# RMSNorm on one core: loads and stores in fewer, larger transfers, three of them split into 27 and 5 rows, with the direction changes tied to landings

## The chip, the cores and the metric

The kernel runs on one core of a Trainium2 chip. The metric is device time in microseconds (us); lower is better. All transfers go over one hardware queue that SyncE (SP in the profile) feeds and that 16 DMA engines serve. The compute is split over ScalarE (ACT), VectorE (DVE) and GpSimd (POOL); TensorE (PE) only spreads gamma over the partitions once.

## What is computed

```python
def setup_inputs():
    batch, seq, dim = 16, 1024, 512
    return {"x": np.random.randn(batch, seq, dim).astype(np.float32),
            "gamma": np.ones(dim, dtype=np.float32)}

def reference(x, gamma):
    eps = 1e-5
    rms = np.sqrt(np.mean(x ** 2, axis=-1, keepdims=True) + eps)
    return (x / rms * gamma).astype(np.float32)
```

There are 16384 rows of 512 floats, 33.55 MB in and 33.55 MB out. Every row is divided by its own root mean square and multiplied by gamma.

## The kernel before

The 16384 rows are four tiles of 128 partitions x 32 rows x 512 floats. A "row" below is one row on every partition: 128 x 2 KB = 256 KB. Partition p of a tile holds 32 consecutive rows of x, so a transfer of n rows moves n x 2 KB of contiguous memory for each partition. There are three SBUF slots (64 KB a partition each); tiles 0, 1, 2 and 3 use slots 0, 1, 2 and 0 (`slot_of`). The results overwrite x in its slot, so tile 3 can only be loaded when tile 0 has been stored.

The work goes in groups of rows, written as `(tile, first row, rows, pieces, POOL's share)`. For each group:

- `square_sums` (L89 to L99): for each piece, ACT squares the rows into a scratch (L96) and DVE sums over the 512 columns (L97). A piece of 9 rows uses rows 23 to 31 of slot 2 as its scratch, as long as tile 2 is not there. Other pieces alternate between a PSUM scratch of 7 rows and an SBUF scratch of 5.
- `inverse_rms` (L101 to L104): ACT takes the root of sum/512 + eps (L102), DVE the reciprocal (L103).
- `scale_by_pool` (L106 to L113): POOL does the last `share` rows of the group by itself, first times the reciprocal (L109), then times gamma (L110).
- `scale` (L115 to L118): ACT multiplies the other rows by their reciprocals, one instruction a row.
- `times_gamma` (L120 to L127): DVE multiplies the same rows by gamma, in one instruction (L122).

The schedule is written by hand: each engine runs its instructions in the order of the program. The main loop (L166 to L182) goes one group ahead: while group k is scaled, group k + 1 is squared and summed; the reciprocals of group k + 1 follow the gamma product of group k on DVE.

All DMAs are issued by SP in the order of the program: `load` (L45), `store` (L49) and gamma's pieces (L58). The loads of tile 0 and half of tile 1 come first, then each group's `transfers` (L129 to L149). SP waits at each for what it needs: a load into a slot for the last readers of those rows, a store for DVE's and POOL's results. While SP waits, every later transfer waits with it, but the DMA engines go on with what is already queued.

Of the kernel before, what the change touches and what calls it, by code (L numbers as in the profile page):

```python
# [9 lines left out]
def kernel(  # L10
# [14 lines left out]
    of = out.flatten_outer_dims()  # L25
    N, D = xf.shape
# [17 lines left out]
    def load(t, slot, r0, r1):  # L44
        dma = nc.sync.dma_start(out=slots[slot][:, r0:r1], in_=xv[t][:, r0:r1])  # L45
        before_scale.append((slot, r0, r1, dma))

    def store(t, slot, r0, r1):
        dma = nc.sync.dma_start(out=ov[t][:, r0:r1], in_=slots[slot][:, r0:r1])  # L49
        before_scale.append((slot, r0, r1, dma))  # L50

    gamma_row = const.tile([1, D], fp32)
    pieces = (0, 128, 224, 320, 416, D)

    load(0, 0, 0, 1)
    load(0, 0, 1, 8)
    for c0, c1 in zip(pieces, pieces[1:]):
        nc.sync.dma_start(out=gamma_row[:, c0:c1], in_=gamma.unsqueeze(0)[:, c0:c1])  # L58
    load(0, 0, 8, 16)
    load(0, 0, 16, 32)  # L60
    load(1, 1, 0, 16)

    ones_col = const.tile([1, P], fp32)
    nc.gpsimd.memset(ones_col, 1.0)  # L64
# [9 lines left out]


    groups = [
        (0, 0, 7, (7,), 3),
        (0, 7, 9, (9,), 5),
        (0, 16, 16, (7, 9), 7),
        (1, 0, 16, (7, 9), 7),  # L80
        (1, 16, 16, (7, 5, 4), 7),
        (2, 0, 16, (7, 5, 4), 7),
        (2, 16, 16, (7, 5, 4), 7),
# [36 lines left out]
    def times_gamma(t, g, r0, r1):  # L120
# [4 lines left out]
        for slot, b0, b1, earlier in before_scale:  # L125
            if slot == slot_of[t] and b0 < g + r1 and g + r0 < b1:
                tc.declare_no_dep(scaled.ins, earlier.ins, reason="ScalarE waited for it before it scaled these rows")  # L127

    def transfers(t, g):  # L129
        if (t, g) == (0, 0):  # L130
            store(0, 0, 0, 1)
            load(1, 1, 16, 32)
            store(0, 0, 1, 2)
            load(2, 2, 0, 23)
        elif (t, g) == (0, 16):
            store(0, 0, 2, 3)
            load(2, 2, 23, 32)
            store(0, 0, 3, 16)
            store(0, 0, 16, 32)
            load(3, 0, 0, 16)  # L140
            load(3, 0, 16, 32)
        elif (t, g) == (1, 16):
            store(1, 1, 0, 32)
        elif (t, g) == (2, 16):
            store(2, 2, 0, 32)
        elif (t, g) == (3, 0):
            store(3, 0, 0, 16)
        elif (t, g) == (3, 16):
            store(3, 0, 16, 32)  # L149
# [16 lines left out]
    for k, group in enumerate(groups):  # L166
        t, g, n, pieces, share = group
        mine = n - share
        half = (mine + 1) // 2
        ahead = groups[k + 1 :][:1]  # L170
        ss, todo = pieces_of(ahead[0]) if ahead else (None, [])
        scale_by_pool(rstd, t, g, n, share)
        for piece in todo[:2]:
            square_sums(*piece)
        scale(rstd, t, g, 0, half)
        for piece in todo[2:]:
            square_sums(*piece)
        scale(rstd, t, g, half, mine)
        times_gamma(t, g, 0, mine)
        transfers(t, g)  # L180
        for nxt in ahead:
            rstd = inverse_rms(ss, nxt[2])  # L182
# [30 lines left out]
```

## Time and profile before

| | |
|---|---|
| time, median of 3 runs | 161.68 us (161.65 to 161.87) |
| span of the profiled execution, first to last instruction | 160.2 us (160.165) |
| bytes moved | 67.12 MB, a mean of 419 GB/s over the span |
| busy share | DVE 70%, ACT 67%, POOL 66%, PE 1% |
| busy share of the 16 DMA engines | 98.1% |
| DMA packets | 2747 |

The profiled execution's own time is not given apart from its span; the median of the runs is 1.5 us above the span, which is what lies before the first and after the last instruction. In the profile, "idle before, releaser" says how long an engine stood still before an instruction and what ended it. In the windows the columns are the window and its length, then busy time and number of instructions of PE, PEld (weight load), DVE, ACT and POOL, the clock granted to TensorE, the busy share of the DMA engines and the GB/s that they moved. In the timeline the columns are start, duration, engine, line, operation, and output from input; SPq are the DMA issues of SP.

### The profile page before, as it was taken

Reading aid. Unit: us, or ns where it says so; the run is one execution under the profiler, and the core shown is the slowest. Engines: PE = TensorE matmul, PEld = TensorE weight load, DVE = VectorE, ACT = ScalarE, POOL = GpSimd, SP = SyncE. Lnnn points to the kernel's source line nnn. Section 1 sums busy time; section 2 is a strip of 40 time slices with the busy share of each in tenths; the row PEclk is TensorE's granted clock in tenths of the full one; section 3 lists DMA queues with packets and bytes.
Section 4 is the critical chain, followed back from the end, with each engine's and each line's share of the span. In section 5 each row is a group of like instructions: output and inputs, shape, how many; then the busy total and the mean of one; then the engine's idle time right before and its main releaser. Section 6 shows DMA issues by size and latency. Waiting matters only on the chain.

```text
span 160.2 us, 276 instructions
## 1 busy us (share of the span) xinstructions
PE 2.0 (1%) x2; PEld 0.5 (0%) x2; DVE 112.0 (70%) x39; ACT 107.8 (67%) x108; POOL 106.4 (66%) x24
## 2 busy tenths in 40 slices
PE   0050000000000000000000000000000000000000
PEld 0010000000000000000000000000000000000000
DVE  0018098899798999999999999999999009700000
ACT  3071967976999998999899899989960990000000
POOL 1000951994999599999999999999999980000000
DMA  5999999899999899999999999996996996999994
GB/s 189 431 421 475 442 401 458 340 446 491 417 435 494 388 379 383 426 450 475 434 401 426 483 401 393 524 491 295 524 491 295 524 491 295 401 491 417 401 450 196
DMA packets 2747, 67.12 MB, mean 419 GB/s; under 512 B 313, under 2 KB 314, under 8 KB 826
## 3 DMA queue, kind: packets, MB, share of 16 engines
q1 hardware_dynamic: 2746, 67.11, 98.1%
q14 instruction: 1, 0.01, 0.0%
HBM read 33.56 MB, written 33.55 MB: 419 GB/s over the span
## 4 chain that ended last, share of the span: by engine, by line
DVE 59%; ACT 22%; DMA 4%; ACTq 0%; issue 0%; SPq 0%
DVE ss L97 36%; DVE slot L122 23%; ACT slot L118 8%; ACT slot L96 7%; ACT sq_psum L96 6%; DMA slot<-in_x_dram 4%; DVE ss L103 1%; ACT ss L102 1%; ACTq L208 0%; ACT gamma_b L165 0%; SPq L45 0%; ACTq L96 0%
## 5 line engine op out<-in xcount | busy, mean ns | idle before, releaser
L109 POOL TENSOR_TENSOR slot<-slot,ss 128x3584 f32<-128x3584 f32 (+2 forms) x9 | 47.0, 5218 | 24.1 <-DVE ss L103 24.1
L110 POOL TENSOR_TENSOR slot<-slot,gamma_b 128x3584 f32<-128x3584 f32 (+2 forms) x9 | 59.3, 6587 | 0.7
L97 DVE TENSOR_REDUCE ss<-sq_psum 128x7 f32<-128x3584 f32 (+1 forms) x13 | 42.2, 3247 | 13.7 <-ACT sq_psum L96 13.7
L118 ACT ACTIVATE slot<-slot,ss 128x512 f32<-128x512 f32 x75 | 47.3, 706 | 4.7 <-DVE ss L103 4.7
L122 DVE TENSOR_TENSOR slot<-slot,gamma_psum 128x4608 f32<-128x4608 f32 (+2 forms) x9 | 41.3, 4590 | 8.7 <-ACT slot L118 8.7
L96 ACT ACTIVATE sq_psum<-slot 128x3584 f32<-128x3584 f32 (+1 forms) x13 | 34.6, 2658 | 6.4 <-DMA slot<-in_x_dram 5.7
L97 DVE TENSOR_REDUCE ss<-slot 128x9 f32<-128x4608 f32 x3 | 14.9, 4954 | 4.4 <-ACT slot L96 4.2
L97 DVE TENSOR_REDUCE ss<-sq_sbuf 128x5 f32<-128x2560 f32 x5 | 14.0, 2803 | 0.0
L96 ACT ACTIVATE slot<-slot 128x4608 f32<-128x4608 f32 x3 | 12.1, 4033 | 0.0
L96 ACT ACTIVATE sq_sbuf<-slot 128x2560 f32<-128x2560 f32 x5 | 11.6, 2321 | 0.0
L102 ACT ACTIVATE ss<-ss,eps_t 128x16 f32<-128x16 f32 (+2 forms) x9 | 2.7, 305 | 11.9 <-DVE ss L97 11.9
L103 DVE RECIPROCAL ss<-ss 128x16 f32<-128x16 f32 (+2 forms) x9 | 2.1, 236 | 0.4 <-ACT ss L102 0.4
L66 PE MATMUL gamma_psum<-gamma_row,ones_col 1*128 1x512 f32 x2 | 2.0, 1122 | 8.6 <-DMA gamma_row<-in_gamma_dram 8.6
L72 ACT ACT_TABLE_LOAD x1 | 1.3, 1283 | 1.2 <-PEq L197 1.2
L165 ACT COPY gamma_b<-gamma_psum 128x512 f32<-128x512 f32 x1 | 0.6, 567 | 0.0
L66 PEld LDWEIGHTS gamma_psum<-gamma_row,ones_col 1*128 1x128 f32 x2 | 0.5, 308 | 8.6 <-issue 8.6
L64 POOL MEMSET ones_col<- 1x128 f32 x1 | 0.2, 195 | 0.3 <-POOLq L197 0.3
L197 POOL MEMSET const-float32-0.0<- 128x1 f32 x1 | 0.1, 99 | 0.2 <-issue 0.2
L72 ACT ACTIVATE table<-eps_t 128x1 f32<-128x1 f32 x1 | 0.2, 202 | 0.0
L197 POOL MEMSET const-bfloat16-1.0<- 128x1 bf16 x1 | 0.1, 102 | 0.0
L197 POOL MEMSET const-uint8-127<- 128x1 uint8 x1 | 0.1, 102 | 0.0
L197 POOL MEMSET const-float32-1.0<- 128x1 f32 x1 | 0.1, 99 | 0.0
(1 smaller groups left out, 0.1 us busy)
## 6 DMA issues: line engine op xcount, KB each, us to landing
slot<-in_x_dram SPq DMA_DIRECT2D x5, 4096.0 KB, 21.9
out_dram<-slot SPq DMA_DIRECT2D x3, 4096.0 KB, 23.4
slot<-in_x_dram SPq DMA_DIRECT2D x1, 5888.0 KB
out_dram<-slot SPq DMA_DIRECT2D x1, 3328.0 KB, 21.8
slot<-in_x_dram SPq DMA_DIRECT2D x1, 2304.0 KB, 14.3
slot<-in_x_dram SPq DMA_DIRECT2D x1, 2048.0 KB, 9.9
slot<-in_x_dram SPq DMA_DIRECT2D x1, 1792.0 KB, 7.0
out_dram<-slot SPq DMA_DIRECT2D x3, 256.0 KB
```

The source lines that it names most:

```text
L66: nc.tensor.matmul(gamma_psum[:, 0], ones_col, gamma_row, start=True, stop=True)
L72: nc.scalar.activation(out=table, in_=eps_t, func=AF.Sqrt)
L96: nc.scalar.activation(out=sq[:, :m], in_=rows, func=AF.Square)
L97: nc.vector.tensor_reduce(out=ss[:, r : r + m, 0], in_=sq[:, :m], axis=mybir.AxisListType.X, op=OP.add)
L102: nc.scalar.activation(out=ss[:, :n, 0], in_=ss[:, :n, 0], func=AF.Sqrt, bias=eps_t, scale=1.0 / D)
L103: nc.vector.reciprocal(out=ss[:, :n, 0], in_=ss[:, :n, 0])
L109: nc.gpsimd.tensor_tensor(out=part, in0=part, in1=by_row, op=OP.mult)
L110: last = nc.gpsimd.tensor_tensor(out=part, in0=part, in1=gamma_b.to_broadcast([P, share, D]), op=OP.mult)
L118: nc.scalar.activation(out=x[:, g + r, :], in_=x[:, g + r, :], func=AF.Copy, scale=rstd[:, r])
L122: scaled = nc.vector.tensor_tensor(out=part, in0=part, in1=gamma_psum.to_broadcast([P, r1 - r0, D]), op=OP.mult)
L165: nc.scalar.copy(out=gamma_b[:, 0], in_=gamma_psum[:, 0])
L197: nc = _bacc.Bacc("TRN2", target_bir_lowering=False, num_devices=1)
```

## The change

The transfers are cut differently and the groups with them.

- The first half of tile 0 is loaded in one transfer of 16 rows, not in 1, 7 and 8, and the first two groups (7 and 9 rows) become one of 16 rows.
- Gamma's row comes in 2 pieces, not 5.
- The second half of tile 1 is loaded at the start and not after the first store.
- Tile 2 is loaded as 27 + 5 rows, not 23 + 9; the three stores of one row between the loads are gone; tile 0 is stored as 27 + 5 rows and tile 3 loaded as 27 + 5.
- The group (1, 0) takes pieces of 7, 5 and 4 rows, not 7 and 9, since its scratch rows in slot 2 are overwritten earlier.
- Two stores get an additional wait: the store of tile 0 for the landing of the first 27 rows of tile 2, and the store of tile 1 for that of the first 27 rows of tile 3. The load of the first 27 rows of tile 3 waits, as before, until the rows of slot 0 that it overwrites are stored.

```diff
@@ load and store
     def load(t, slot, r0, r1):
         dma = nc.sync.dma_start(out=slots[slot][:, r0:r1], in_=xv[t][:, r0:r1])
         before_scale.append((slot, r0, r1, dma))
+        return dma
 
-    def store(t, slot, r0, r1):
+    def store(t, slot, r0, r1, behind=None):
         dma = nc.sync.dma_start(out=ov[t][:, r0:r1], in_=slots[slot][:, r0:r1])
         before_scale.append((slot, r0, r1, dma))
+        if behind is not None:
+            tc.add_manual_dep(
+                dma.ins,
+                behind.ins.name,
+                mybir.DependencyInfo(mybir.DependencyClass.Sync, mybir.DependencyReason.DATA),
+                reason="the queue gets this store when the load ahead of it is nearly through",
+            )
 
-    pieces = (0, 128, 224, 320, 416, D)
-
-    load(0, 0, 0, 1)
-    load(0, 0, 1, 8)
+    pieces = (0, 256, D)
+
+    load(0, 0, 0, 16)
     for c0, c1 in zip(pieces, pieces[1:]):
         nc.sync.dma_start(out=gamma_row[:, c0:c1], in_=gamma.unsqueeze(0)[:, c0:c1])
-    load(0, 0, 8, 16)
     load(0, 0, 16, 32)
     load(1, 1, 0, 16)
+    load(1, 1, 16, 32)
@@ groups
-        (0, 0, 7, (7,), 3),
-        (0, 7, 9, (9,), 5),
+        (0, 0, 16, (7, 9), 7),
         (0, 16, 16, (7, 9), 7),
-        (1, 0, 16, (7, 9), 7),
+        (1, 0, 16, (7, 5, 4), 7),
         (1, 16, 16, (7, 5, 4), 7),
@@ transfers
+    last_load = {}
+
     def transfers(t, g):
         if (t, g) == (0, 0):
-            store(0, 0, 0, 1)
-            load(1, 1, 16, 32)
-            store(0, 0, 1, 2)
-            load(2, 2, 0, 23)
+            last_load[2] = load(2, 2, 0, 27)
+            load(2, 2, 27, 32)
         elif (t, g) == (0, 16):
-            store(0, 0, 2, 3)
-            load(2, 2, 23, 32)
-            store(0, 0, 3, 16)
-            store(0, 0, 16, 32)
-            load(3, 0, 0, 16)
-            load(3, 0, 16, 32)
+            store(0, 0, 0, 27, behind=last_load[2])
+            store(0, 0, 27, 32)
+            last_load[3] = load(3, 0, 0, 27)
+            load(3, 0, 27, 32)
         elif (t, g) == (1, 16):
-            store(1, 1, 0, 32)
+            store(1, 1, 0, 32, behind=last_load[3])
         elif (t, g) == (2, 16):
             store(2, 2, 0, 32)
```

## The prediction, made before the changed kernel ran

> **What bounds the kernel now.** I read the page first: spans and queues.
>
> ```profile
> span 160.2 us, 276 instructions
> ...
> PE 2.0 (1%) x2; PEld 0.5 (0%) x2; DVE 112.0 (70%) x39; ACT 107.8 (67%) x108; POOL 106.4 (66%) x24
> ...
> DMA packets 2747, 67.12 MB, mean 419 GB/s; under 512 B 313, under 2 KB 314, under 8 KB 826
> ...
> q1 hardware_dynamic: 2746, 67.11, 98.1%
> ```
>
> No compute engine is busy over 70% of the span; the 16 DMA engines are at 98.1% on one queue. The critical chain names DVE for 59%, but it follows instructions, not the queue behind them. So the second view is the timeline of SP, which issues every transfer, and then DVE's last line in the whole timeline.
>
> ```profile
> 0.74 0.86 SPq L45 DMA_DIRECT2D slot<-in_x_dram  x2
> ...
> 27.35 0.35 SPq L49 DMA_DIRECT2D out_dram<-slot  x1
> 27.74 0.43 SPq L45 DMA_DIRECT2D slot<-in_x_dram  x1
> ...
> 50.25 5.48 SPq L49 DMA_DIRECT2D out_dram<-slot  x2
> 72.09 10.27 SPq L45 DMA_DIRECT2D slot<-in_x_dram  x2
> 83.64 55.90 SPq L49 DMA_DIRECT2D out_dram<-slot  x4
> ```
>
> ```profile
> 132.05 7.09 DVE L122 TENSOR_TENSOR slot<-slot,gamma_psum 128x6656 f32<-128x6656 f32 x1 [8.13 <-ACT slot L118]
> ```
>
> The last store is issued at 139.2 us, when DVE ends, and lands 20.1 us later. Its own 4.19 MB take 9.7 us, so some 10 us of older stores stood before it. Compute is ahead; the bound is the DMA stream, 1.75 us (first packet) to 158.99 (last): 157.24 us.
>
> Third, the stream itself, packet by packet in the trace's DMA records. A transfer is 128 packets, 8 to each engine. An undisturbed packet takes 81 ns for 1 row, 533 for 7, 611 for 8, 686 for 9, 987 for 13, 1213 for 16, 1740 for 23, 2418 for 32. That is 75.4 ns a row and about 6 a packet, loads and stores alike. By these the 19 transfers of x are 155.44 us an engine, and 9 ns for each of 19 semaphore packets make 155.61. The other 1.63 us are losses: about 0.5 of slower packets in the first 6 us, a start staggered by up to 0.4, and 0.87 of load packets slowed 1 to 3 us before some loads give way to a store (0.26 us an engine near 29 to 31 us, 0.38 near 61 to 63, 0.22 near 99; none before the store row at 42 us, 0.01 at 55). The windows show two of these as dips and the long stores after 100 us at full rate (packets are booked where they start, so neighbours blur):
>
> ```profile
> 28.00:32.00 4.00, 0.00 (x0) 0.00 (x0) 3.45 (x1) 4.00 (x2) 3.98 (x1) 1.00 0.87 346
> ...
> 60.00:64.00 4.00, 0.00 (x0) 0.00 (x0) 4.00 (x2) 3.63 (x5) 3.92 (x2) 1.00 1.04 406
> ...
> 100.00:158.00 58.00, 0.00 (x0) 0.00 (x0) 31.00 (x11) 26.00 (x33) 31.57 (x6) 1.00 1.00 434
> ```
>
> **Fewer, larger transfers.** There are 14 transfers of x, not 19. A 27-row packet is 23 rows plus 4 x 75.4 = 2042 ns, a 5-row one 533 - 2 x 75.4 = 382. Per engine: loads of tiles 0 and 1 are 4 x 8 x 1213 = 38.82 us; load 2, store 0 and load 3 are 8 x 2424 = 19.39 each; stores 1 and 2 are 19.34 each; store 3 is 16 x 1213 = 19.41. Sum 155.09, with 14 x 9 ns 155.22: **0.40 us less**. Gamma moves in 2 pieces, not 5, of 22 to 27 ns each on one engine: nothing, since x's packets surround them. The first packet still comes 1.0 us after the first issue; the 0.5 us of slow start may be 0.3 to 0.6 with 32 KB packets; I keep 0.5.
>
> The Trainium skill (DMA: Bandwidth & Descriptors, Anatomy of one DMA) fits a DMA of its software path as 2.0 us plus bytes over 436 GB/s. Were that paid in series, the 8 transfers saved (gamma's included) would be an estimated 16 us.
>
> In this trace a queued transfer's packets begin 2 ns after the last one's end (31.766 to 31.768), so nothing is paid in series and the 0.40 stands.
>
> **Switches between load and store.** Five load-to-store switches cost 0.87 together; two remain. Such a switch cost 0 to 0.38 here, so two cost 0 to 0.8. I take 0.3 each, the mean of the two that precede a long store (0.38, 0.22): 0.6, **0.27 less**.
>
> **The added waits.** Three times SP now waits for a landing with only 5 rows (8 x 382 = 3.06 us) still queued: store 0 behind load 2's 27 rows, load 3 behind store 0's 27 rows (slot reuse), store 1 behind load 3's 27 rows. The loop: the slowest engine's last packet to landing is 0.36 us for loads (7.90 to 8.22, 32.42 to 32.78), up to 0.61 after a store (81.39 to 82.00); SP issues 0.02 later (82.02); issue to first packet is 1.0 us on the first engine and 1.4 on the last (0.74 to 1.75 and 2.14, the only issue into an empty queue). Sum 1.4 to 2.05 us. Engines end 0.65 to 0.9 us apart, so the fastest has 2.15 to 2.4 us. Covered by 0.1 to 1.0 us: I price it at nothing. Without cover, an uncovered microsecond costs one, plus about 0.45 of slow first packet (first packets took 468 to 581 ns instead of 81). From below the price can be minus 0.6, the whole switch loss, if it comes from stores queued too early. Queued behind SP's waits are only the transfers in their order; no compute engine waits on SP except through landings.
>
> The skill (same page, Rules for kernel authors) says to issue a DMA early and wait late, which speaks against these waits. With its 2.0 us of fixed cost as the loop, an estimate, 3.06 - 0.9 = 2.16 us still cover it, and the sum stands.
>
> **What the compute does with it.** Squares start when 16 rows are in. Rows 0 to 15 were in at 13.12 before; say 12.9, so ACT starts at 13.0. Squares 3.16, the second 3.96, reduce 4.96, root and reciprocal 0.6: 25.6. gamma copy 0.47, squares 3.05 + 3.96, reduce 4.96: DVE frees the scratch rows of slot 2 at 38.0. Load 2 now needs that in whole (before, 23 rows went without). The queue is empty at about 41.5 (42.75 before, less one store row 0.67, a switch 0.26 and smaller savings); first packets at 39.0 to 39.4: covered by 1.4 to 1.8 us after the spread of engines.
> Store 0's 27 rows need POOL's share of group (0, 16): reciprocal at 43.7 (scales end 38.5, gamma product 4.95, reciprocal 0.25), POOL 14.05: 57.8. Load 2's 27 rows land at 41.5 + 16.3 + 0.36 = 58.2. POOL is just in time; nothing.
> So DVE's chain is 2.5 us later than before (reciprocal of group (1, 0) at 57.8, before 55.24). One cover goes: ACT's square at 91.77 found rows of tile 3 that had landed at 91.5. Now it would start at 94.3, but 27 rows land together at about 97.1, so ACT waits some 3 us and DVE 2. The final product ends at 139.15 + 2.5 + 2.5 = 144. The stores before it keep the queue busy to 148; after wake, issue and spread 1.7 to 3 us of cover remain (now about 8). Nothing.
>
> **Sum.** 157.24 - 0.40 - 0.27 = 156.57, 0.67 us less. Median 161.68 against a span of 160.17: 1.5 us lie around the span and stay. 161.68 - 0.67 = **161.0 us**. The measurement can tell 0.2% (0.32 us) from no change.
>
> **Rivals.**
> *Slower: the turnarounds run dry.* At the three waits the queue must be refilled within about 2.2 us. For it: my margin is as low as 0.1 us, issue latency is seen once, and slow packets 1 to 3 us ahead of a switch suggest that engines look ahead about that far. Against: the rows above. Price: it decides from the point where the loop passes 2.2 us. At 2.4 us it costs three times 0.2 + 0.45 = 1.95 in place of the 0.6 of the switches: 161.0 + 1.35 = 162.35. I put it at 162.4; at 2.6 us it would be 162.95.
> *Same: the savings are eaten.* Each turn exposes only the slow first packet, 3 x 0.45 = 1.35 where I have 0.6: 161.0 + 0.75 = 161.75.
> *Compute becomes the end.* It decides from 3 us more delay than I have in DVE's chain (another late landing at 80 or 97 us): each further us costs one; 162.5.
> *The wait is idle.* If a store queued early is what slows the loads and the wait cures it, both switches cost 0: 160.4. If the wait changes nothing there, my forecast holds.
>
> **How the numbers follow.** Forecast with the cure 0.58 (160.2 to 161.35), same 0.18, dry turns 0.17, late compute 0.07. So faster 0.58, same 0.18, slower 0.24. Low end: no switch loss and a start loss of 0.3: 161.0 - 0.6 - 0.2 = 160.2. The high end stops at 162.4, inside the dry turns; about 2 in 10 is left out in all.
>
> **What would show it.** 14 x 128 + 14 x 16 + 4 + 1 = 2021 DMA packets; DMA share at 98% or more; SP issuing store 0 at about 58.2, load 3 at 78, store 1 at 97; a last store issued near 144 and landing some 14 us later; a new wait of ACT on a load of slot of about 3 us. I am wrong if engines idle around 60, 80 or 99 us, if load 2 is issued after 41 us, or if the last store lands less than 11 us after its issue.

## The result and the profile after

The changed kernel took 162.80 us (median of 5 runs, 162.08 to 163.20) against 161.68 (161.63 to 161.87) for the kernel before: a ratio of 1.006, 95% interval 1.0043 to 1.0078. It became slower by about 1 us where 0.67 us less was forecast. Two later groups gave 1.0045 (1.0022 to 1.0068) and 1.0053 (1.0024 to 1.0083); over all 29 runs its median is 162.48 us, while the kernel before had 161.50 to 161.54 in every later group. The profiled execution after took 162.08 us with a span of 160.3, so it shows the fastest of these five runs, not a usual one.

The page of the changed kernel, spans and queues:

```profile
span 160.3 us, 255 instructions
...
PE 2.0 (1%) x2; PEld 0.5 (0%) x2; DVE 112.6 (70%) x38; ACT 108.3 (68%) x109; POOL 104.1 (65%) x22
...
DMA packets 2021, 67.12 MB, mean 419 GB/s; under 512 B 226, under 2 KB 228, under 8 KB 228
...
q1 hardware_dynamic: 2020, 67.11, 97.7%
```

The packets are the 2021 that were worked out, 726 fewer than before, and yet the mean rate is the same 419 GB/s and the busy share of the DMA engines is lower, 97.7%. Something else takes back what the packets save. Next, the timeline of SP in the changed kernel (start, duration, what is issued):

```profile
1.80 36.88 SPq L45 DMA_DIRECT2D slot<-in_x_dram  x5
58.59 0.82 SPq L50 DMA_DIRECT2D out_dram<-slot  x2
78.12 3.76 SPq L45 DMA_DIRECT2D slot<-in_x_dram  x2
98.53 47.09 SPq L50 DMA_DIRECT2D out_dram<-slot  x4
```

Load 2 is issued in time: its 27 rows, the fourth of the five loads in the line of 1.80, go out at 37.87. Store 0 goes out at 58.59, load 3 at 78.12 and store 1 at 98.53; 58.2, 78 and 97 were forecast. The last is 1.5 us late, and the chain of work that ended last shows where that comes from:

```profile
58.53 0.03 SPq L50
58.56 0.03 issue
58.59 19.51 DMA out_dram<-slot
78.10 0.02 issue
78.12 20.29 DMA slot<-in_x_dram
98.42 0.02 issue
98.44 0.02 ACT sq_psum L102
```

From store 0's landing to the issue of load 3 there are 20 ns, from load 2's to store 0's about 70. But load 3's 27 rows land 20.29 us after their issue. They had 2.1 us of queue ahead of them (first packet at 80.26) and are 8 x 2041 ns = 16.3 us long, 0.4 us more with the landing: 18.8 us. The other 1.5 us are the subject of the experiments.

### The profile page after: what moved, and what is told of

It is laid out like the page before. It is cut to its first block, busy times and chain, and to the rows that moved or that the text cites. A ratio compares the mean times of both kernels' runs of the same rounds, so it can differ in the third digit from the quotient of the medians.

```text
span 160.3 us, 255 instructions
## 1 busy us (share of the span) xinstructions
PE 2.0 (1%) x2; PEld 0.5 (0%) x2; DVE 112.6 (70%) x38; ACT 108.3 (68%) x109; POOL 104.1 (65%) x22
## 2 busy tenths in 40 slices
DMA packets 2021, 67.12 MB, mean 419 GB/s; under 512 B 226, under 2 KB 228, under 8 KB 228
## 3 DMA queue, kind: packets, MB, share of 16 engines
q1 hardware_dynamic: 2020, 67.11, 97.7%
## 4 chain that ended last, share of the span: by engine, by line
DMA 45%; DVE 22%; ACT 20%; issue 2%; ACTq 0%; SPq 0%
DMA slot<-in_x_dram 33%; DMA out_dram<-slot 12%; DVE ss L103 12%; DVE slot L128 11%; ACT slot L124 8%; ACT sq_psum L102 5%; ACT slot L102 5%; ACT sq_sbuf L102 1%; ACTq L212 0%; ACT gamma_b L169 0%; DVE ss L109 0%; ACT ss L108 0%; SPq L50 0%
## 5 line engine op out<-in xcount | busy, mean ns | idle before, releaser
L115 POOL TENSOR_TENSOR slot<-slot,ss 128x3584 f32<-128x3584 f32 (+1 forms) x8 | 45.9, 5738 | 31.4 <-DVE ss L109 31.4
L103 DVE TENSOR_REDUCE ss<-sq_psum 128x7 f32<-128x3584 f32 (+1 forms) x14 | 44.5, 3177 | 23.2 <-ACT sq_psum L102 23.2
L116 POOL TENSOR_TENSOR slot<-slot,gamma_b 128x3584 f32<-128x3584 f32 (+1 forms) x8 | 58.0, 7247 | 0.6
L128 DVE TENSOR_TENSOR slot<-slot,gamma_psum 128x4608 f32<-128x4608 f32 (+1 forms) x8 | 41.7, 5213 | 8.9 <-ACT slot L124 8.9
L103 DVE TENSOR_REDUCE ss<-sq_sbuf 128x5 f32<-128x2560 f32 x6 | 16.8, 2802 | 0.0
L102 ACT ACTIVATE sq_sbuf<-slot 128x2560 f32<-128x2560 f32 x6 | 13.9, 2322 | 0.0
L103 DVE TENSOR_REDUCE ss<-slot 128x9 f32<-128x4608 f32 x2 | 9.9, 4953 | 0.1
L102 ACT ACTIVATE slot<-slot 128x4608 f32<-128x4608 f32 x2 | 8.1, 4029 | 0.0
L108 ACT ACTIVATE ss<-ss,eps_t 128x16 f32<-128x16 f32 x8 | 2.4, 305 | 7.8 <-DVE ss L103 7.8
L109 DVE RECIPROCAL ss<-ss 128x16 f32<-128x16 f32 x8 | 2.0, 244 | 0.4 <-ACT ss L108 0.4
```

The lines of the kernel that those rows point to most:

```text
L102: nc.scalar.activation(out=sq[:, :m], in_=rows, func=AF.Square)
L103: nc.vector.tensor_reduce(out=ss[:, r : r + m, 0], in_=sq[:, :m], axis=mybir.AxisListType.X, op=OP.add)
L108: nc.scalar.activation(out=ss[:, :n, 0], in_=ss[:, :n, 0], func=AF.Sqrt, bias=eps_t, scale=1.0 / D)
L109: nc.vector.reciprocal(out=ss[:, :n, 0], in_=ss[:, :n, 0])
L115: nc.gpsimd.tensor_tensor(out=part, in0=part, in1=by_row, op=OP.mult)
L116: last = nc.gpsimd.tensor_tensor(out=part, in0=part, in1=gamma_b.to_broadcast([P, share, D]), op=OP.mult)
```

## How the losses are counted

Every packet record of the trace has a start and a duration, and every size an undisturbed duration, its most frequent one (2041 ns for 27 rows, 385 for 5, 84 for 1). The packets' sum is that of the transfers of x by these durations, per engine. The loss in a stretch is its length less the undisturbed work done in it, per engine, as a mean over the 16 engines. "Stagger" is what the engines lose as a mean because they run out of work before the last of them does. All in us; "quartiles" are those of the run times, one profiled run each, and the last columns are windows of time in us.

A ratio below compares a kernel with the kernel before run beside it; it lies nearer to the means than to the medians, so a few runs of the kernel before at 163 us and more weigh in it. "Bootstrap" is a 95% interval for the difference of two medians, found by drawing the runs again at random. Some of these differences are between groups run at different times, in which the kernel before had the same 161.50 to 161.53 us.

| kernel | median | quartiles | profiled | packets' sum | 0-6 | 28-34 | 46-56 | 56-66 | 76-88 | 94-104 | stagger |
|---|---|---|---|---|---|---|---|---|---|---|---|
| before, first profile | 161.68 | 161.65-161.77 | span 160.2 | 155.48 | 0.82 | 0.24 | 0 | 0.34 | 0 | 0.21 | 0.46 |
| before again | 161.54 | 161.46-162.08 | 161.34 | 155.48 | 0.83 | 0.22 | 0 | 0.08 | 0 | 0 | 0.17 |
| changed | 162.80 | 162.59-162.90 | 162.08 | 155.14 | 0.86 | 0 | 0.22 | 0.08 | 0.39 | 0 | 0.89 |
| changed, again | 162.27 | 162.02-162.74 | 162.04 | 155.14 | 0.76 | 0 | 0 | 0.18 | 0.44 | 0.02 | 0.95 |
| changed, third | 162.44 | 162.28-162.97 | 162.00 | 155.14 | 0.83 | 0 | 0 | 0.22 | 0.38 | 0.02 | 0.88 |
| no waits | 164.24 | 163.38-164.57 | 164.41 | 155.14 | 0.78 | 0 | 0.03 | 0.96 | 0.51 | 0.62 | 1.91 |
| halves | 161.95 | 161.82-162.09 | 162.16 | 155.14 | 0.82 | 0 | 0.12 | 1.00 | 0 | 0.09 | 0.33 |
| before, short turn | 161.91 | 161.69-162.38 | 162.37 | 155.48 | 0.83 | 0.20 | 0 | 0.28 | 0.16 | 0.18 | 0.82 |
| old start | 162.22 | 161.89-162.52 | 161.97 | 155.27 | 0.76 | 0 | 0 | 0.06 | 0.41 | 0 | 0.88 |
| deep turn, 16 rows | 161.73 | 161.53-162.20 | 161.65 | 155.20 | 0.82 | 0 | 0.16 | 0.04 | 0.16 | 0 | 0.72 |
| turn of 10 rows | 161.83 | 161.76-162.10 | 161.86 | 155.21 | 0.75 | 0 | 0 | 0.08 | 0.55 | 0 | 0.71 |
| deep turn, old start | 161.55 | 161.51-162.20 | 162.24 | 155.34 | 0.78 | 0 | 0 | 0.04 | 0.22 | 0.02 | 1.07 |
| deep, no waits | 162.10 | 162.07-162.14 | 162.09 | 155.20 | 0.78 | 0 | 0 | 1.14 | 0 | 0.02 | 0.41 |
| turn of 3 rows | 162.00 | 161.86-162.17 | 161.91 | 155.14 | 0.80 | 0 | 0 | 0.12 | 1.04 | 0 | 0.36 |
| deep, wait on store 0 | 162.74 | 162.28-163.11 | 163.25 | 155.20 | 0.82 | 0 | 0 | 0.18 | 0.29 | 1.19 | 1.00 |
| before, both waits | 162.47 | 161.97-162.85 | 162.19 | 155.61 | 0.79 | 0.24 | 0 | 0 | 0.02 | 0.02 | 0.77 |
| the same, again | 162.67 | 162.34-162.98 | 161.70 | 155.61 | 0.77 | 0.21 | 0 | 0 | 0 | 0 | 0.25 |
| before, wait on store 1 | 161.83 | 161.77-161.90 | 161.83 | 155.61 | 0.80 | 0.26 | 0 | 0.16 | 0 | 0 | 0.26 |
| one row store | 161.57 | 161.49-161.68 | 161.68 | 155.21 | 0.85 | 0 | 0.24 | 0.40 | 0 | 0.14 | 0.28 |
| two row stores | 161.74 | 161.65-161.80 | 161.63 | 155.34 | 0.81 | 0 | 0.36 | 0.16 | 0 | 0 | 0.25 |

## The experiments

### Which part costs

**Without the two added waits.** `store(0, 0, 0, 27)` and `store(1, 1, 0, 32)` without `behind`.

```diff
-            store(0, 0, 0, 27, behind=last_load[2])
+            store(0, 0, 0, 27)
...
-            store(1, 1, 0, 32, behind=last_load[3])
+            store(1, 1, 0, 32)
```

> The changed kernel without its two added waits; store 0 is queued as soon as its rows are ready (about 57.9 us) and store 1 near 86 us, early. Theory A (a turn with only 5 rows queued lets single engines stumble, and the stumble reaches the end): two of three such turns are gone, only load 3 behind store 0's 27 rows is left; 162.2 us, between the changed kernel's 162.8 and the 161.7 of before, and a narrower spread of runs. Theory B (the larger first load and the later compute cost the time): no change, 162.8. Theory C (the waits help, as stores queued early slow the loads): slower than 162.8.

Measured: 164.24 us (162.83 to 164.68), 1.0139 (1.009 to 1.0189) of the kernel before: slower than the changed kernel. Store 0 was issued at 57.60 in place of 58.59, and the stretch around 60 us lost 0.96 us an engine in place of 0.08 to 0.22; near 99 us it was 0.62 in place of 0 to 0.02. So theory C holds in part: in this cut the waits do what they were made for, and taking both out does not give back what the change costs. The loss at 76 to 88 us stayed (0.51).

**Halves in place of 27 + 5**, waits kept.

```diff
-            last_load[2] = load(2, 2, 0, 27)
-            load(2, 2, 27, 32)
+            last_load[2] = load(2, 2, 0, 16)
+            load(2, 2, 16, 32)
...
-            store(0, 0, 0, 27, behind=last_load[2])
-            store(0, 0, 27, 32)
-            last_load[3] = load(3, 0, 0, 27)
-            load(3, 0, 27, 32)
+            store(0, 0, 0, 16, behind=last_load[2])
+            store(0, 0, 16, 32)
+            last_load[3] = load(3, 0, 0, 16)
+            load(3, 0, 16, 32)
```

> The changed kernel with load 2, store 0 and load 3 cut into 16 + 16 rows in place of 27 + 5; the two added waits stay, now each with 16 rows (9.7 us) queued behind what they wait for. Theory A (too little is queued at the turns): 161.2 us or less, the runs within 0.3 us. Theory B (start and compute): 162.8, or a little less, since tile 3's first rows land earlier. Theory C (switches themselves cost, however deep the queue): 162.5.

Measured: 161.95 us, ratio 1.0005 (0.9978 to 1.0033), the runs within 0.6 us; the median is 0.42 us over that of the kernel before. Theory A is right that the depth matters (the loss at 76 to 88 us is gone, the stagger falls from 0.88 or more to 0.33), but its 161.2 is missed: the switch at 60 us now costs 1.00 us, and store 0 is queued at 51.8, 9 us ahead of it.

**The short turn alone, in the kernel before.**

```diff
-            store(0, 0, 3, 16)
-            store(0, 0, 16, 32)
-            load(3, 0, 0, 16)
-            load(3, 0, 16, 32)
+            store(0, 0, 3, 27)
+            store(0, 0, 27, 32)
+            load(3, 0, 0, 27)
+            load(3, 0, 27, 32)
```

> The kernel before with one part of the change alone: store 0 ends in 24 + 5 rows and load 3 comes in 27 + 5 (13 + 16 and 16 + 16 before), so load 3 is issued with 5 rows queued. No added wait, old start. Theory A: one of the three short turns; 161.9 to 162.2 us with runs that differ by over 0.3 us. Theory B: 161.7.

Measured: 161.91 us, ratio 1.0033 (1.0001 to 1.0065), half of the runs spread over 0.7 us (0.2 in the kernel before beside it). A 0.4 us dearer median and a wide scatter come from this one edit. The trace, of a run of 162.37, has 0.16 us at 76 to 88 us, where both profiles of the kernel before have none, and a stagger of 0.82.

**The old start in the changed kernel** (1 + 7 + 8 rows, five gamma pieces, first groups of 7 and 9 rows).

```diff
-    load(0, 0, 0, 16)
+    load(0, 0, 0, 1)
+    load(0, 0, 1, 8)
...
-        (0, 0, 16, (7, 9), 7),
+        (0, 0, 7, (7,), 3),
+        (0, 7, 9, (9,), 5),
```

> The changed kernel with the start of before: tile 0's first half in 1 + 7 + 8 rows, gamma in 5 pieces, first groups of 7 and 9 rows. The short turns and the added waits stay. Theory A: 162.8, unless the earlier compute matters. Theory B (start and later compute cost): 161.7 to 162.0, and the part of the time that lies outside the span, 1.8 us in the changed kernel and 1.5 in that before, goes back to 1.5.

Measured: 162.22 us, ratio 1.0023 (0.9991 to 1.0054). Against all 29 runs of the changed kernel that is 0.26 us less, with a bootstrap interval of -0.14 to 0.74: not settled, and not the 0.8 or more of theory B. Both starts lose 0.76 to 0.86 us. The part of the time outside the span was 1.8 us in both kernels and in this one (1.8 to 2.0 in all profiles); the 1.5 of theory B, which also stands ahead of the prediction, came from setting a profiled span against the median of other runs.

### The turn from store 0 to load 3

**The changed kernel again**, beside the next three.

> The changed kernel as it is, beside the next ones on one chip, for a second profile of it. Both theories: about 1 us over the kernel before. Theory A2 (the turn from store 0 to load 3, with only 5 rows queued, slows the first packet of load 3 on each engine by up to 1 us, and the slowest engine carries that to the end): the trace again shows 0.3 to 0.5 us lost per engine between 80 and 84 us, and engines that end load 3 over 1 us apart. Theory B (start, later compute): no such loss, or one that moves about.

Measured: 162.27 us, 1.0045 (1.0022 to 1.0068); 0.44 us lost at 76 to 88 us and engines that end 1.5 us apart (157.57 to 159.06).

**The turn made deep, 16 rows.**

```diff
-            store(0, 0, 0, 27, behind=last_load[2])
-            store(0, 0, 27, 32)
-            last_load[3] = load(3, 0, 0, 27)
+            store(0, 0, 0, 16, behind=last_load[2])
+            store(0, 0, 16, 32)
+            load(3, 0, 0, 16)
+            last_load[3] = load(3, 0, 16, 27)
             load(3, 0, 27, 32)
```

> The changed kernel with only the turn from store 0 to load 3 made deep: store 0 goes in 16 + 16 rows and load 3 in 16 + 11 + 5, so load 3's first part is issued with 16 rows (9.7 us) queued. The two load-to-store turns keep their waits and their 5 rows. Theory A2: no loss between 80 and 84 us, engines end 0.6 to 0.8 us apart; 1 us faster than the changed kernel and 0.3 to 0.7 faster than the kernel before, about 161.0 us. Theory B: as the changed kernel. Theory C (the short load-to-store turns hurt as well): between the two.

Measured: 161.73 us, ratio 1.0024 (1.0001 to 1.0047). The 161.0 that theory A2 expected is missed. The median is 0.54 us less than that of the changed kernel beside it (bootstrap -0.06 to 1.12, which alone settles nothing) and 0.74 less than that of all its runs (0.14 to 1.12). The windows of the same 12 us, the kernel before (second profile), the changed one (third profile) and this one, in this order (last column GB/s; packets are booked where they start):

```profile
76.00:88.00 12.00, 0.00 (x0) 0.00 (x0) 12.00 (x5) 11.35 (x12) 12.00 (x2) 1.00 0.97 418
```

```profile
76.00:88.00 12.00, 0.00 (x0) 0.00 (x0) 12.00 (x5) 11.44 (x13) 11.92 (x3) 1.00 0.97 404
```

```profile
76.00:88.00 12.00, 0.00 (x0) 0.00 (x0) 12.00 (x5) 11.44 (x13) 11.92 (x3) 1.00 1.01 431
```

The changed kernel moves least. The packet records of that kernel say how: the first load packet after the turn took up to 1012 ns more than its 2041 (profile after), 1519 in the second and 1139 in the third.

The deep turn makes this smaller but does not end it. There it is store 0's last packet that runs long, by up to 0.98 us on one engine, and 0.16 us an engine and 0.72 of stagger are left. Two other kernels with this turn and a wait on store 0 lost 0.22 and 0.29 us there, in runs over their medians; without the waits the same turn lost nothing. The edit also made load 3's first packets smaller (16 rows in place of 27), and no run separates that from the depth of the queue.

ACT no longer waits for load 3 either. The wait views, changed kernel first, then the deep turn:

```profile
ACT sq_psum L102 <- DMA slot<-in_x_dram: 15.1, 2, 10.3
```

```profile
ACT sq_psum L102 <- DMA slot<-in_x_dram: 10.2, 1, 10.2
```

The 4.9 us of ACT that go are not what the time gains, since the last store was issued at 145.28 in the changed kernel while the queue was full to 148.08.

**A turn of 10 rows** (store 0 in 22 + 10, load 3 in 22 + 5 + 5).

```diff
-            store(0, 0, 0, 27, behind=last_load[2])
-            store(0, 0, 27, 32)
-            last_load[3] = load(3, 0, 0, 27)
+            store(0, 0, 0, 22, behind=last_load[2])
+            store(0, 0, 22, 32)
+            load(3, 0, 0, 22)
+            last_load[3] = load(3, 0, 22, 27)
```

> The same with the turn at 10 rows (6.0 us): store 0 in 22 + 10, load 3 in 22 + 5 + 5. It asks how deep the queue must be. Theory A2 with a look-ahead of 2 to 3 us: no loss, the same time as with 16 rows. If any change from store to load that SP issues late costs, whatever is queued: a loss in between, 0.1 to 0.3 us per engine near 80 us.

Measured: 161.83 us, ratio 1.0023 (1.0006 to 1.004). The trace still lost 0.55 us, most of it in the store's last packets. Time and trace do not agree on one edge.

**A turn of 3 rows** (store 0 in 29 + 3, the rest as changed).

```diff
-            store(0, 0, 0, 27, behind=last_load[2])
-            store(0, 0, 27, 32)
+            store(0, 0, 0, 29, behind=last_load[2])
+            store(0, 0, 29, 32)
```

> The changed kernel with the turn from store 0 to load 3 at 3 rows (1.8 us): store 0 in 29 + 3, the rest as it is. Theory A2 with a hard edge (the queue runs empty when the cover is under the 1.7 to 2 us from an engine's last packet to the next one's first): idle engines near 80 us, 0.5 us or more on top of the changed kernel, 163 or more. If it is the switch and not the depth: as the changed kernel, 162.3.

Measured: 162.00 us, ratio 1.0035 (1.0018 to 1.0053): the hard edge of theory A2 is refuted. The mean loss did rise as it should, to 1.04 us with idle engines (0.24) among it, but all 16 engines' first load packets ran long, by 0.4 to 1.1 us, and the stagger is 0.36 in place of 0.88 to 0.95. Mean loss and stagger together are 1.40 us, against 1.26 to 1.39 in the changed kernel.

**The deep turn with the old start**: the edits of the deep turn and of the old start together.

```diff
-    load(0, 0, 0, 16)
+    load(0, 0, 0, 1)
+    load(0, 0, 1, 8)
...
+            load(3, 0, 0, 16)
+            last_load[3] = load(3, 0, 16, 27)
```

> The deep turn of 16 rows with the start of before (1 + 7 + 8 rows, five gamma pieces, first groups of 7 and 9). Theory A2: the same time as the deep turn alone within 0.2 us, since both starts lost about 0.8 us. Theory B: 0.5 us or more faster than the deep turn alone.

Measured: 161.55 us, ratio 0.9999 (0.997 to 1.0028): level with the kernel before; 0.19 us under the deep turn alone, with a bootstrap interval that spans zero (-0.54 to 0.69).

### The waits, one by one

**The deep turn without waits** (this edit and the next are shown against the deep turn).

```diff
-            store(0, 0, 0, 16, behind=last_load[2])
+            store(0, 0, 0, 16)
...
-            store(1, 1, 0, 32, behind=last_load[3])
+            store(1, 1, 0, 32)
```

> The kernel with the deep turn of 16 rows (store 0 in 16 + 16, load 3 in 16 + 11 + 5), without either added wait: store 0 is queued near 57.6 us, store 1 near 86. Theory W (a store queued over 3 us before the loads end slows the last loads by 0.2 to 1 us per engine, and the waits avoid that): 0.7 to 1.5 us slower than with the waits (161.7), and the trace shows 0.5 us or more lost near 60 and near 100 us. Rival (in the run without waits and with the short turn it was the short turn that made 164.2): no slower than 161.7.

Measured: 162.10 us, ratio 1.0033 (1.0024 to 1.0043), half of the runs within 0.07 us. It lost 1.14 us around 60 us and nothing near 100, though store 1 was queued early too, at 85.6. The rival is half true as well: 2 us of the 164.2 without waits came with the short turn (164.24 against 162.10).

**The deep turn with the wait on store 0 alone.**

```diff
-            store(1, 1, 0, 32, behind=last_load[3])
+            store(1, 1, 0, 32)
```

> The deep turn of 16 rows with the wait on store 0 alone; store 1 is queued near 86 us, some 14 us before the loads end. Theory W: between the two waits and none; the trace loses under 0.15 us near 60 and 0.2 to 0.7 near 100; 0.2 to 0.6 us slower than with both. Rival: as with both waits, 161.7.

Measured: 162.74 us, ratio 1.0068 (1.0045 to 1.0092). The profile is of a run of 163.25. The first loss was not removed but moved: 0.18 around 60 us, 1.19 near 100, where store 1, queued at 85.7, was now the first long store to be queued early. With both waits the two are 0.04 and 0, and 161.73 us.

**The kernel before with both waits**, twice (shown against the kernel before).

```diff
-            load(2, 2, 23, 32)
-            store(0, 0, 3, 16)
+            last_load[2] = load(2, 2, 23, 27)
+            load(2, 2, 27, 32)
+            store(0, 0, 3, 16, behind=last_load[2])
...
-            load(3, 0, 16, 32)
+            last_load[3] = load(3, 0, 16, 27)
+            load(3, 0, 27, 32)
...
-            store(1, 1, 0, 32)
+            store(1, 1, 0, 32, behind=last_load[3])
```

> The kernel before with the two added waits alone: load 2 in 23 + 4 + 5 rows and store 0 behind the 4, load 3 in 16 + 11 + 5 and store 1 behind the 11; its start, its three stores of one row and its deep turn from store 0 to load 3 stay. Theory W: the losses near 61 us (0.38) and 99 us (0.22) fall to 0.1 or less; 161.0 to 161.2 us against 161.5, faster than both kernels. Rival (a wait anywhere makes the engines drift apart): 161.5 or slower, with engines that end 1 us apart.

> The kernel before with both added waits, again. The first profile was of a run of 162.19, under its median, and showed no loss at 61 and 99 us. Theory S: median 0.5 to 1 us over the kernel before, and if the profile falls in a run of 162.5 or more, its loss lies at the two waits (61 or 99 us) or in engines that end over 1 us apart. Theory W (the waits only help): 161.3 or less.

Measured: 162.47 us (162.32 without one run of 164.65), ratio 1.005 (1.0031 to 1.007), and 162.67, 1.0061 (1.0032 to 1.009). Both traces show what theory W says, no mean loss at 61 and 99 us, and the time is 0.8 to 1.2 us worse all the same. In the first profile, of a run of 162.19, the engines drift apart as the rival said: the last to finish a transfer is 0.41 us behind the first before the turn from store 0 to load 3, 0.82 behind it at the end of store 0 and 1.01 after the switch near 99. In the second, of 161.70, the two stay 0.4 apart. Both runs are under the median, so what the slower runs lose is not seen.

**The same with the wait on store 1 alone.**

```diff
-            store(0, 0, 3, 16, behind=last_load[2])
+            store(0, 0, 3, 16)
```

> The kernel before with the same cuts as with both waits, but only store 1 waits (for load 3's rows 16 to 26). Theory S: one late switch in place of two: half of the extra time, 161.8 to 162.1 us, and a scatter between the two. Theory W: 161.5 or less.

Measured: 161.83 us, ratio 1.0011 (0.9987 to 1.0035), half of the runs within 0.13 us. So the wide scatter of both waits comes with the one on store 0: 0.84 us between the two medians (bootstrap 0.25 to 1.17). The issue of store 0's two parts, with both waits (first profile) and with the one on store 1:

```profile
60.65 0.82 SPq L50 DMA_DIRECT2D out_dram<-slot  x2
```

```profile
50.68 5.00 SPq L50 DMA_DIRECT2D out_dram<-slot  x2
```

### The kernels' usual runs

**Both kernels once more.**

> The kernel before, unchanged, for a second profile of it beside the others. Its runs lie at 161.5 us with spans of 159.7; the first profile had a span of 160.2, so it may not show a usual run. Theory S (deeply queued switches cost little and the same in each run; switches that SP issues within some 3 us of need hit single engines by up to 1.5 us, differently in each run, and the slowest engine sets the end): a profile of span 159.7 shows engines that end within 0.7 us of each other and 0.4 us less loss than the first. Theory N (the chip's own noise): as scattered as the others.

> The changed kernel again, for its scatter and a third profile. Theory S: median 0.6 to 1.1 us over the kernel before, half of its runs spread over 0.5 us or more; the loss lies at 80 to 84 us and in the stagger at the end. Theory N: the scatter of the kernel before on this chip.

Measured: 161.54 and 162.44 us, the second with a ratio of 1.0053 (1.0024 to 1.0083). The page of the second profile of the kernel before, a run of 161.34 us:

```profile
span 159.6 us, 276 instructions
...
DMA packets 2747, 67.12 MB, mean 421 GB/s; under 512 B 313, under 2 KB 314, under 8 KB 826
...
q1 hardware_dynamic: 2746, 67.11, 98.2%
```

The first profile, with its 160.2, was of a slower run than most: it lost 0.34 and 0.21 us at 61 and 99 us and had 0.46 of stagger; here the three are 0.08, 0 and 0.17. This run is one of the fastest (median 161.54, quartiles 161.46 and 162.08). The changed kernel's third profile is of a run under its lower quartile as well (162.00 against 162.28).

### The stores of one row

**One and two of them back**, in the changed kernel with halves and without waits.

```diff
+            load(2, 2, 0, 16)
+            store(0, 0, 0, 1)
+            load(2, 2, 16, 32)
...
+            store(0, 0, 1, 16)
+            store(0, 0, 16, 32)
+            load(3, 0, 0, 16)
+            load(3, 0, 16, 32)
```

> The changed kernel's start and groups, no added wait, all of load 2, store 0 and load 3 in halves, and one store of one row (tile 0, row 0) between the halves of load 2. Theory F (the first switch from loads to stores that is queued early costs about 1 us per engine when a long store follows, as near 60 us in the two kernels that queue it early without the row stores, but only 0.25 when it is a store of one row, and the later long one then costs under 0.4): 0.2 to 0.4 us lost near 50 us, under 0.4 near 60, time 161.3 to 161.6, with little scatter. Rival: the rows do nothing; 1 us lost near 60 us, time 162.0 to 162.2.

> The same with two stores of one row, between 16, 8 and 8 rows of load 2. Theory F: the long switch near 60 us costs 0.1 or less, the second row store nothing; 161.2 to 161.5 us, at or under the kernel before. Rival: as with one, 162.0 to 162.2.

Measured: 161.57 us, ratio 1.0000 (0.9978 to 1.0022), and 161.74, ratio 1.0003 (0.998 to 1.0027), half of the runs within 0.2 us in both. The kernel with one row store is 0.53 us faster than the deep kernel without waits (bootstrap 0.41 to 0.63), and 0.38 faster than the halves with waits (0.18 to 0.59). Neither pair differs in the row store alone: against the first, loads 2 and 3 are cut in halves as well; against the second, the waits are gone. The windows around the first long switch, the deep kernel without waits first, then the one with a row store:

```profile
56.00:66.00 10.00, 0.00 (x0) 0.00 (x0) 10.00 (x6) 9.35 (x12) 9.92 (x3) 1.00 0.90 341
```

```profile
56.00:66.00 10.00, 0.00 (x0) 0.00 (x0) 10.00 (x6) 9.35 (x12) 9.92 (x3) 1.00 0.98 406
```

341 against 406 GB/s; by the packet records 1.14 us lost against 0.40, with 0.24 paid at the row store. The second row store (between `load(2, 2, 16, 24)` and `load(2, 2, 24, 32)`) takes the long switch to 0.16 and costs 0.36 at the rows: 0.17 us slower in all. None of these kernels is faster than the kernel before beyond its interval.

## Why the prediction was wrong

**The bound** held: the stream of packets begins at 1.74 us and ends at 159.1 in the changed kernel, compute is never the end, and the last store is issued at 145.28 (144 forecast) with 14.2 us to its landing.

**Fewer packets** held: the packets' sum fell from 155.48 to 155.14, 0.34 us an engine and some 0.39 with the semaphore packets, where 0.40 was forecast. (The packet times that the prediction lists add up to 155.37, not to its 155.44; with the measured 84 ns for one row and 535 for seven they give 155.48.)

**The term that failed is the price of the added waits, nothing, above all that of the turn from store 0 to load 3.** The working of the cover was right. Load 3 was issued at 78.12 and its first packet ran at 80.26, so the queue had 2.1 us, over the 1.0 to 1.4 it needs; engines stood idle for at most 0.08 us there. But the first load packet ran up to 1 to 1.5 us long although it was queued in time, on some engines and not on others. In three profiles this is 0.38 to 0.44 us an engine and 0.88 to 0.95 of stagger, where the kernel before has 0 and 0.17 in its second profile. I had priced idle time and an uncovered first packet and took a covered one to be free. With a deep turn (16 rows) the median was 0.5 to 0.7 us lower; the short turn alone, in the kernel before, cost 0.4. The same term put the wait on store 0 at nothing: in the kernel before, with store 1's wait, it cost 0.8 to 1.2 us, and store 1's alone 0.3 (a ratio that does not clear 1). In the deep turn of the changed cut both waits are there and the time is within 0.3 us of the kernel before, so this price is not a fixed one, and what it is in the changed kernel is not shown.

**Means hid the rest.** The sum was made per engine, as if all engines lost alike. The end is set by the slowest. In the changed kernel one engine ends load 3 up to 1.6 us behind another (96.41 to 97.99 in the third profile), and nothing later gives that back. The drift arises at this turn: in the three profiles the last engine to end store 0 is 0.6 to 0.9 us behind the first, the last to end load 3's 27 rows 1.4 to 1.65, and the last to end the kernel still 1.4 to 1.5.

**The base was a slower run than most.** I took 157.24 us of stream and 0.87 of switches from one profile. The second profile, near the fastest, has 156.59 (1.74 to 158.33) and some 0.36 of switches (0.22 at the first row store, 0.06, 0.08), so 0.27 was most of what there was to save. The changed kernel's own load-to-store switches lost 0.08 to 0.24, less than the 0.6 of the forecast: the cure was real, and what it could cure was small.

**The row stores** were priced at 6 ns a packet and one switch. They seem to do more: without them, the first long store that is queued early costs about 1 us (0.96 to 1.19 in four traces), with one or more ahead of it 0.08 to 0.40. The changed kernel escapes that only through its waits. Most kernels with a wait that holds store 0 back scatter widely, but so does the changed cut without waits (quartiles 163.38 and 164.57).

The Trainium skill (DMA: Bandwidth & Descriptors, Rules for kernel authors) asks, for the most bandwidth, for 1 MiB or more in a DMA. These runs do not bear that out for every transfer: a store of one row is 256 KB, and the kernel with one was 0.38 and 0.53 us faster than the two nearest without.

Put together for the second profile of the kernel before and the third of the changed one: -0.34 packets, -0.28 switches at 31 and 42 us, +0.14 around 60, +0.38 at the turn, +0.71 stagger: +0.61 of the 0.71 us between their last packets (158.33 and 159.04). The other 0.2 to 0.4 us up to the medians lie in runs that no profile of the changed kernel caught; I leave their place open.

**The rivals.** The dry turns, priced at 162.4, came nearest in time and place. But the queue was not dry; the packets were slow. The eaten savings had that mechanism, a slow first packet at 0.45 us a turn; it showed at one turn of three, with 0.38 to 0.44 us an engine, and that the engines lose unequally was not in their 161.75. The idle wait was half right, in that the waits do remove the switch loss. Late compute was not it: ACT waited 4.9 us for load 3 (3 forecast), and DVE's end stayed covered.

**What stays open:** why a first load packet runs long when it was queued 1 us ahead, and whether the depth of the queue or the size of the packet sets how long; why the first early long store costs 1 us, and whether a row store alone softens it; why the second one cost 0.62 us without waits in the short turn and nothing in the deep one; why the wait on store 0 scatters the runs and the one on store 1 does not.

## What to carry to other kernels

Where one queue is busy 98% of the span, merging transfers saves a few nanoseconds a packet; what mattered here is what happens where the direction changes. Try more queue at a change from stores to loads (here 16 rows or 10 us took off most of the loss, though not all), and look at when the first and the last engine end, not at the mean. Before costing an edit of under 1%, take more than one profile, or set its span against those of the other runs.

## What the hardware showed that I had not expected

A packet that is queued about 1 us before its engine is free is not safe: in the three profiles of the changed kernel the longest first load packet after a store, of 55 KB, took 3.1 to 3.6 us in place of 2.04, and those on some other engines 2.04. With 16 rows queued it was the store's last packet that ran long, by up to 0.98 us. A loss that hits all 16 engines alike (1.04 us with 3 rows queued) cost no more than one that hits some of them (0.4 us with 5 rows). And in the kernel with a single store of one row, 8 packets of 84 ns an engine, a later switch cost 0.40 us in place of 1.00 to 1.14.
